# A feed-forward block's input on Trainium2: shift of odd tiles and one weight remainder on GpSimd, later statistics for the second half, another order within each product

## The chip, the core and the metric

The kernel runs on one core of a Trainium2 chip. A core has TensorE (matrix products), VectorE and ScalarE (elementwise work), GpSimd (elementwise work too) and SyncE, which issues most DMA transfers. The metric is the time of one execution on the device in microseconds (us); the lower the better.

## The reference, cut to what matters

The model has two layers on 256 latent tokens `x` and 256 context tokens `z`, with 1024 features. Each layer is a half-step feed-forward block, a token mixing, and a second half-step feed-forward block.

```python
def rms_norm(x): return x * lax.rsqrt(mean(x * x, axis=-1) + EPS)
def modulate(h, shift, scale): return h * (1.0 + scale) + shift
def swiglu(h, w1, w3, w2): return (silu(h @ w1) * (h @ w3)) @ w2      # D_FF = 2816

for l in range(2):
    last = l == 1
    x = x + 0.5 * mx[2] * swiglu(modulate(rms_norm(x), mx[0], mx[1]), ffn1_w1[l], ffn1_w3[l], ffn1_w2[l])
    z = z + 0.5 * mz[2] * swiglu(modulate(rms_norm(z), mz[0], mz[1]), ffn1_w1[l], ffn1_w3[l], ffn1_w2[l])
    hx, hz = (modulate(rms_norm(x), mx[3], mx[4]) @ w_in[l], modulate(rms_norm(z), mz[3], mz[4]) @ w_in[l])
    mix_x, mix_z = token_mixing(hx, hz, ...)      # Fourier, neighbourhood attention, GLA, grouped attention
    x = x + mx[5] * (mix_x @ w_out[l])
    x = x + 0.5 * mx[8] * swiglu(modulate(rms_norm(x), mx[6], mx[7]), ffn2_w1[l], ffn2_w3[l], ffn2_w2[l])
    if not last: ...                              # the same two steps for z
return x
```

`mx` and `mz` are nine vectors of 1024 (shift, scale and gate of each block), computed from `c` and `c_ctx` by a matrix product. The token mixing is not touched by the change other than where it calls the common product.

## The kernel before

**Layout.** The state stands transposed in SBUF: eight tiles `X[d]` of 128 features by 512 columns. Columns 0 to 255 are the latents (first half, `s = 0`), 256 to 511 the context (second half, `s = 1`). The second feed-forward block of layer 1 works on the latents alone.

**Products in three parts.** All large products are made at near-f32 precision out of rounded operands (`fp32r`). Of a weight tile `raw` (128 x 1024, streamed in by SyncE's DMA queue in the order of `wlist`, three buffers), ScalarE casts the rounded high part `whi` (line 234) and VectorE subtracts for the remainder `wlo` (line 237). The activations stand as `hh` and `hl` in the same way. `mm3` (lines 278 to 280) then gives `product` (line 266; the matmul is line 271) three matmuls for each product: `whi` by `hh`, `whi` by `hl`, `wlo` by `hh`. Weights are prepared up to `LEAD = 2` ahead of use.

**The feed-forward block.** `ffn` (line 386) handles 22 tiles of 128 hidden features in two groups of 12 and 10. The first two tiles of a block, each with a `w1` and a `w3` product, so four weights, are interleaved: first all products of both tiles for the latents, and then all for the context. So the first products need the latents' tiles `hh0`, `hl0`, `hh1`, ... one after the other, and the context's only later. After that each product is 512 columns wide. The block's last two output tiles are done half by half (`SPLIT = 2`), so that the latents' state is complete earlier; `out_proj` of the mixing (line 1052) does the same (`SPLITO = 2`).

**From one block into the next.** After each output tile `norm_square` (line 283) squares it on ScalarE (`sq`) and adds it to the running sum `ss`, on GpSimd (line 298), for the last tile on VectorE. When a half's last tile is done, `norm_stat` (line 303) is called after a number of further products: a matmul with ones sums over the features (line 310), VectorE scales it to `ms` (line 318), GpSimd raises it to the power -0.5, `rs` (line 320). Some products later `norm_bcast` (line 324) spreads `rs` over the partitions with two transposes into the PSUM tile `pb` (line 327). The table `LAGS` holds both numbers for the two halves: `((6, 6), (4, 4))` means statistics 6 products after a half's last square, broadcast 4 products after that, for either half; its keys 3, 6 and 0 are the block that is entered (mixing, second and first feed-forward block). Where only the latents are computed, there are no lags.

Then `norm_apply_` (line 339) makes the activation tiles of the half, d = 0 to 7, through four buffers `htmp`: VectorE forms `htmp` = X times scale times `pb` (line 347), and ScalarE adds the shift and rounds for `hh` (line 349). For an even tile VectorE makes `hl` from `htmp`, shift and `hh` in one instruction (line 354). For an odd tile (`POOLD`) ScalarE adds the shift to `htmp` in place (line 351), and GpSimd subtracts `hh` (line 352).

**What sets the order.** The program is written unit by unit. A scheduler, which holds its own simulated timeline, puts the instructions of each engine in order, by priority (`tc.high_priority`), and the products are kept behind statistics and broadcasts by `issue_after` and `keep_in_program_order`. Each engine then executes its list strictly in that order. Beside all this VectorE works through `mod_module` (line 159), the vectors of the later blocks, as background work pinned behind the `wlo` instruction recorded last.

## Time and profile before

| | before |
|---|---|
| device time, three runs | 1767.90, 1768.75, 1769.67 us |
| their median | 1768.75 us |
| the profiled execution | 1767.38 us |
| its span in the profile | 1765.6 us |
| granted TensorE clock, mean over the span | 0.989 of full |
| share of the span busy: TensorE, VectorE, ScalarE, GpSimd | 97%, 62%, 38%, 12% |

The profile is of one execution. The span runs from its first to its last recorded instruction; the device time of the same execution is 1.8 us longer. An engine's busy share is a mean over the whole program, in which the feed-forward blocks and the mixing alternate. The granted clock tells at which share of its full speed TensorE was allowed to run.

### The profile page before, as it was taken

Reading aid. Unit: us, or ns where it says so; the run is one execution under the profiler, and the core shown is the slowest. Engines: PE = TensorE matmul, PEld = TensorE weight load, DVE = VectorE, ACT = ScalarE, POOL = GpSimd, SP = SyncE. Lnnn points to the kernel's source line nnn. Section 1 sums busy time; section 2 is a strip of 40 time slices with the busy share of each in tenths; the row PEclk is TensorE's granted clock in tenths of the full one; section 3 lists DMA queues with packets and bytes.
Section 4 is the critical chain, followed back from the end, with each engine's and each line's share of the span. In section 5 each row is a group of like instructions: output and inputs, shape, how many; then the busy total and the mean of one; then the engine's idle time right before and its main releaser. Section 6 shows DMA issues by size and latency. Waiting matters only on the chain.

```text
span 1765.6 us, 27971 instructions
## 1 busy us (share of the span) xinstructions
PE 1708.3 (97%) x11142; PEld 1477.1 (84%) x11142; DVE 1100.2 (62%) x1832; ACT 667.3 (38%) x1122; POOL 216.5 (12%) x259
## 2 busy tenths in 40 slices
PE   7999999999989999999999999999999897999999
PEld 5888888887978788888888888888888796889999
DVE  4577877645876668777333478778733576655554
ACT  4422222235645453222222352222223464554443
POOL 1000000022553230000000110000001344120000
PEclk9999999999999999999999999999999998999999
DMA  9555765333221046655332366567523333136664
GB/s 337 185 186 156 225 203 179 122 94 106 75 62 34 30 150 187 197 166 175 108 98 68 100 212 213 168 198 222 167 81 99 91 103 82 49 124 193 182 190 136
DMA packets 92275, 254.03 MB, mean 144 GB/s; under 512 B 17649, under 2 KB 28145, under 8 KB 91761
## 3 DMA queue, kind: packets, MB, share of 16 engines
q1 hardware_dynamic: 90560, 250.93, 46.0%
q8 instruction: 87, 1.43, 0.3%
q10 hardware_dynamic: 1584, 1.32, 0.2%
q14 instruction: 44, 0.35, 0.1%
HBM read 251.16 MB, written 1.05 MB: 143 GB/s over the span
## 4 chain that ended last, share of the span: by engine, by line
PE 89%; DMA 4%; DVE 3%; ACT 1%; issue 1%; POOL 1%; SPq 0%; POOLq 0%; DVEq 0%; ACTq 0%
PE p L271 48%; PE py L271 23%; PE pt L271 8%; PE pyo L271 3%; DMA bias<-in_na_rpb_dram 2%; PE pf L271 1%; PE po L776 1%; PE prT L767 1%; DVE wlo L237 1%; PE sc L744 1%; DMA wfirst<-in_wmodf_dram 1%; PE pa L660 1%; PE pg L540 0%; ACT whi L234 0%; DMA raw<-in_f1w_dram 0%
## 5 line engine op out<-in xcount | busy, mean ns | idle before, releaser
L234 ACT CAST whi<-raw 128x1024 fp32r<-128x1024 f32 (+3 forms) x358 | 340.0, 951 | 893.5 <-PE p L271 289.2
L237 DVE TENSOR_TENSOR wlo<-raw,whi 128x1024 fp32r<-128x1024 f32 (+3 forms) x358 | 396.6, 1110 | 226.6 <-ACT whi L234 219.0
L271 PE MATMUL p<-hl,whi 128*128 128x512 f32 (+1 forms) x1504 | 527.5, 352 | 2.1 <-DVE hl L354 1.4
L271 PE MATMUL p<-hh,wlo 128*128 128x512 f32 (+1 forms) x1504 | 526.7, 351 | 0.3 <-DVE wlo L237 0.3
L271 PE MATMUL p<-hh,whi 128*128 128x512 f32 (+1 forms) x1504 | 524.9, 352 | 1.9 <-ACT hh L349 1.1
L271 PEld LDWEIGHTS p<-hl,whi 128*128 128x128 f32 x1504 | 285.2, 190 | 40.5 <-DVE hl L354 1.8
L271 PEld LDWEIGHTS p<-hh,whi 128*128 128x128 f32 x1504 | 283.6, 190 | 40.9 <-ACT hh L349 1.9
L271 PEld LDWEIGHTS p<-hh,wlo 128*128 128x128 f32 x1504 | 285.2, 190 | 38.4 <-DVE wlo L237 0.6
L167 DVE CUSTOM_DVE_ANT_0 mprod<-wmod,crow 128x1024 f32<-128x1024 f32 x256 | 301.9, 1218 | 0.0
L271 PE MATMUL py<-gh,whi 128*128 128x512 f32 (+1 forms) x764 | 266.3, 350 | 0.0
L271 PE MATMUL py<-gh,wlo 128*128 128x512 f32 (+1 forms) x764 | 265.7, 348 | 0.0
L271 PE MATMUL py<-gl,whi 128*128 128x512 f32 (+1 forms) x764 | 264.0, 346 | 0.0
L298 POOL TENSOR_TENSOR ss<-ss,sq 128x512 f32<-128x512 f32 (+1 forms) x34 | 40.9, 1202 | 1064.6 <-ACT sq L295 1063.1
L396 DVE TENSOR_TENSOR g<-p,sl 128x512 f32<-128x512 f32 (+1 forms) x88 | 54.9, 624 | 180.6 <-PE p L271 180.1
L271 PEld LDWEIGHTS py<-gh,wlo 128*128 128x128 f32 x764 | 143.4, 188 | 20.5
L271 PEld LDWEIGHTS py<-gl,whi 128*128 128x128 f32 x764 | 143.3, 188 | 19.8
L271 PEld LDWEIGHTS py<-gh,whi 128*128 128x128 f32 x764 | 143.5, 188 | 17.7
L271 PE MATMUL pt<-whi,hl 128*128 128x256 f32 x448 | 132.7, 296 | 9.7 <-POOL hl L352 9.7
L271 PE MATMUL pt<-whi,hh 128*128 128x256 f32 x448 | 132.6, 296 | 1.2 <-ACT nt L518 0.7
L271 PE MATMUL pt<-wlo,hh 128*128 128x256 f32 x448 | 132.3, 295 | 0.0
L466 DVE SCALAR_TENSOR_TENSOR X<-py,mod,X 128x256 f32<-128x256 f32 x112 | 50.3, 480 | 98.6 <-PE py L271 98.5
L271 PEld LDWEIGHTS pt<-whi,hl 128*128 128x128 f32 x448 | 88.7, 198 | 18.5 <-POOL hl L352 12.5
(218 smaller groups left out, 1706.9 us busy)
## 6 DMA issues: line engine op xcount, KB each, us to landing
wmod<-in_wmodt_dram SPq DMA_DIRECT2D x128, 512.0 KB, 3.7
raw<-in_f1w_dram SPq DMA_DIRECT2D x88, 512.0 KB, 4.1
raw<-in_f2w_dram SPq DMA_DIRECT2D x88, 512.0 KB, 4.1
raw<-in_f1w_dram SPq DMA_DIRECT2D x32, 384.0 KB, 3.7
raw<-in_f2w_dram SPq DMA_DIRECT2D x32, 384.0 KB, 3.4
raw<-in_f1w_dram SPq DMA_DIRECT2D x32, 320.0 KB, 2.8
raw<-in_f2w_dram SPq DMA_DIRECT2D x32, 320.0 KB, 2.9
wfirst<-in_wmodf_dram SPq DMA_DIRECT2D x32, 256.0 KB, 5.9
```

Of the source, the lines that this page charges most:

```text
L167: nc.vector.tensor_tensor_reduce(out=prod, in0=raw, in1=crow[:, s], scale=1.0, scalar=0.0, op0=ALU.mult, op1=ALU.add, accum_out=acc[:, s, ...
L234: nc.scalar.copy(hi[:, :k * n], raw[:, :k * n])
L237: wlo[0] = nc.vector.tensor_tensor(out=lo[:, :k * n], in0=raw[:, :k * n], in1=hi[:, :k * n].bitcast(F32), op=ALU.subtract).ins
L271: nc.tensor.matmul(ps, w, x, start=first and i == 0, stop=last and i == len(parts) - 1)
L298: (nc.vector if d == KD - 1 else eng).tensor_tensor(out=st["ss"][:, c], in0=st["ss"][:, c], in1=sq[:, c], op=ALU.add)
L396: nc.vector.tensor_tensor(out=g[:, :n], in0=p3[:, :n], in1=sl[:, :n], op=ALU.mult)
L466: nc.vector.scalar_tensor_tensor(out=X[mt][:, c], in0=py[:, c], scalar=mcol(l, m, mt, s), in1=X[mt][:, c], op0=ALU.mult, op1=ALU.add)
L660: nc.tensor.matmul(pa[w * b:w * b + w, c * w:c * w + w], ke[hs, k0:k0 + w], qe[hs, q0:q0 + w], start=True, stop=True)
L744: nc.tensor.matmul(ps[:, :n], q[:, e, (t % 2) * P:(t % 2 + 1) * P], ks[e][:, T - n:T], start=i == 0, stop=i == 1)
L767: nc.tensor.transpose(pt[:, c * P:(c + 1) * P], pr[e][:, (2 * half + i) * P:(2 * half + i + 1) * P], ident)
L776: last_mm = nc.tensor.matmul(po[64 * e:64 * e + 64, c0:c0 + P], vs[e][4 - nkt + kt], prT[:, (2 * e + i) * P:(2 * e + i + 1) * P], start=kt ...
```

## The change

The diff makes four edits.

1. In `norm_apply_`, the shift of odd tiles goes from ScalarE to GpSimd (`tensor_scalar` with the shift as a column), except on entry to the mixing (`m == 3`) and to the very first block (`l + m == 0`). These are the entries to the second feed-forward block of layer 0 and to the first of layer 1, with two halves, and to the second of layer 1, with the latents alone: 8 + 8 + 4 instructions.
2. In the same three blocks the fourth weight (`w3` of the second tile, noted in `plow`) gets its remainder `wlo` on GpSimd instead of VectorE. That instruction is not recorded in `wlo[0]`.
3. `LAGS` for the entries 6 and 0: the second half's statistics come 14 products after its last square instead of 6.
4. `mm3` takes `wlo` by `hh` second and `whi` by `hl` last. This holds for every product that goes through `mm3`.

```diff
--- before.py
+++ after.py
@@ -23,7 +23,7 @@
 EPS = 1e-6
 LEVELS = (64, 32, 16, 8, 4, 2, 1)
 LEAD = 2
-LAGS = {3: ((6, 6), (4, 4)), 6: ((6, 6), (4, 4)), 0: ((6, 6), (4, 4))}
+LAGS = {3: ((6, 6), (4, 4)), 6: ((6, 14), (4, 4)), 0: ((6, 14), (4, 4))}
 SPLIT = 2
 SPLITO = 2
 SKIP = 4
@@ -178,9 +178,12 @@
 
 
     wlist = []
+    plow = []
 
     def ffn_units(l, f):
         w1, w3, w2 = a[f"f{f}w1"], a[f"f{f}w3"], a[f"f{f}w2"]
+        if l or f == 2:
+            plow.append(len(wlist) + 3)
         for f0, f1 in ((0, FA), (FA, NF)):
             for t in range(f0, f1):
                 wlist.append((w1[l, t], KD, 128))
@@ -218,23 +221,26 @@
     def w_load():
         if pos[0] < len(wlist):
             src, k, n = wlist[pos[0]]
+            low = nc.gpsimd if pos[0] in plow else nc.vector
             pos[0] += 1
             raw = wp.tile([P, 1024], F32, tag="raw", name="raw", bufs=3)
             nc.sync.dma_start(out=raw[:, :k * n], in_=src)
-            loaded.append((raw, k, n))
+            loaded.append((raw, k, n, low))
 
     def w_conv(pool=None, after=None):
         if not loaded:
             w_load()
         if not loaded:
             return
-        raw, k, n = loaded.pop(0)
+        raw, k, n, low = loaded.pop(0)
         tp, nb = (wp, 4) if pool is None else (pool, 1)
         hi = tp.tile([P, 1024], F32R, tag="whi", name="whi", bufs=nb)
         nc.scalar.copy(hi[:, :k * n], raw[:, :k * n])
         lo = tp.tile([P, 1024], F32R, tag="wlo", name="wlo", bufs=nb)
         with tc.issue_after(after) if after is not None else nullcontext():
-            wlo[0] = nc.vector.tensor_tensor(out=lo[:, :k * n], in0=raw[:, :k * n], in1=hi[:, :k * n].bitcast(F32), op=ALU.subtract).ins
+            i = low.tensor_tensor(out=lo[:, :k * n], in0=raw[:, :k * n], in1=hi[:, :k * n].bitcast(F32), op=ALU.subtract).ins
+        if low is nc.vector:
+            wlo[0] = i
         ready.append((hi[:, :k * n].rearrange("p (k n) -> p k n", k=k),
                       lo[:, :k * n].rearrange("p (k n) -> p k n", k=k),
                       raw[:, :k * n].rearrange("p (k n) -> p k n", k=k)))
@@ -277,7 +283,7 @@
 
     def mm3(ps, w, k, xh, xl, first, last):
         wh, wl = w[:2]
-        product(((wh[:, k, :], xh), (wh[:, k, :], xl), (wl[:, k, :], xh)), ps, first, last)
+        product(((wh[:, k, :], xh), (wl[:, k, :], xh), (wh[:, k, :], xl)), ps, first, last)
 
 
     def norm_square(st, pool, d, s0, s1, eng=nc.gpsimd):
@@ -348,7 +354,10 @@
                                            in1=st["pb", s][:, :S], op0=ALU.mult, op1=ALU.mult)
             nc.scalar.activation(hh[:, c], tmp, AF.Identity, bias=mcol(l, m, d, s))
             if d in POOLD[s]:
-                nc.scalar.activation(tmp, tmp, AF.Identity, bias=mcol(l, m, d, s))
+                if m == 3 or l + m == 0:
+                    nc.scalar.activation(tmp, tmp, AF.Identity, bias=mcol(l, m, d, s))
+                else:
+                    nc.gpsimd.tensor_scalar(out=tmp, in0=tmp, scalar1=mcol(l, m, d, s), scalar2=None, op0=ALU.add)
                 nc.gpsimd.tensor_tensor(out=hl[:, c], in0=tmp, in1=hh[:, c].bitcast(F32), op=ALU.subtract)
             else:
                 st["hl", s, d] = nc.vector.scalar_tensor_tensor(out=hl[:, c], in0=tmp, scalar=mcol(l, m, d, s),
```

The scheduler turns this into the following orders. A row is the line of the code, the operation and its tiles (result <- operands, with running numbers) and its size. `ss` is the running sum of squares, `rs` the power, `hl1` to `hl7` the low activations of the odd tiles, `p13` the result of an interleaved product, `pb` the PSUM tile of the statistics. The diff moves line numbers by 4 to 9.

GpSimd on entry to the second feed-forward block of layer 0, before:

```order
L298 TENSOR_TENSOR ss_6152<-ss_6152,sq_6366 128x256
L320 TENSOR_TENSOR rs_6428<-ms_6426,mhalf_94 128x2
L298 TENSOR_TENSOR ss_6152<-ss_6152,sq_6437 128x256
L352 TENSOR_TENSOR hl1_6456<-htmp_6457,hh1_6455 128x256
L352 TENSOR_TENSOR hl3_6469<-htmp_6470,hh3_6468 128x256
L352 TENSOR_TENSOR hl5_6482<-htmp_6483,hh5_6481 128x256
L320 TENSOR_TENSOR rs_6565<-ms_6563,mhalf_94 128x2
L352 TENSOR_TENSOR hl7_6495<-htmp_6496,hh7_6494 128x256
```

GpSimd at the same place, after:

```order
L326 TENSOR_TENSOR rs_6428<-ms_6426,mhalf_94 128x2
L304 TENSOR_TENSOR ss_6152<-ss_6152,sq_6437 128x256
L360 TENSOR_SCALAR htmp_6457<-htmp_6457,mod0_97 128x256
L360 TENSOR_SCALAR htmp_6470<-htmp_6470,mod0_97 128x256
L361 TENSOR_TENSOR hl1_6456<-htmp_6457,hh1_6455 128x256
L241 TENSOR_TENSOR wlo_6540<-raw_6536,whi_6538 128x1024
L361 TENSOR_TENSOR hl3_6469<-htmp_6470,hh3_6468 128x256
L360 TENSOR_SCALAR htmp_6483<-htmp_6483,mod0_97 128x256
L360 TENSOR_SCALAR htmp_6496<-htmp_6496,mod0_97 128x256
L361 TENSOR_TENSOR hl5_6482<-htmp_6483,hh5_6481 128x256
L361 TENSOR_TENSOR hl7_6495<-htmp_6496,hh7_6494 128x256
L326 TENSOR_TENSOR rs_6589<-ms_6587,mhalf_94 128x2
```

Four shifts (line 360) and the fourth weight's remainder `wlo_6540` have come into the row. The remainder stands between `hl1` and `hl3`, two shifts now stand ahead of `hl1`, and the second power `rs_6589`, which stood ahead of `hl7`, now stands behind it.

TensorE at the same entry, around the second half's statistics (the matmul with ones), before:

```order
L271 MATMUL p13_6527<-hh3_6468,whi_6371 128x256
L271 MATMUL p13_6527<-hl3_6469,whi_6371 128x256
L271 MATMUL p13_6527<-hh3_6468,wlo_6373 128x256
L271 MATMUL p13_6527<-hh4_6475,whi_6371 128x256
L310 MATMUL pb_6560<-ones_92,ss_6152 128x1 x2
L271 MATMUL p13_6526<-hh3_6468,whi_6336 128x256
L271 MATMUL p13_6526<-hl3_6469,whi_6336 128x256
L271 MATMUL p13_6526<-hh3_6468,wlo_6338 128x256
```

TensorE around the same statistics, after:

```order
L277 MATMUL p13_6527<-hl6_6489,whi_6371 128x256
L316 MATMUL pb_6584<-ones_92,ss_6152 128x1 x2
L277 MATMUL p13_6526<-hh7_6494,whi_6336 128x256
L277 MATMUL p13_6526<-hh7_6494,wlo_6338 128x256
L277 MATMUL p13_6527<-hh7_6494,whi_6371 128x256
L277 MATMUL p13_6527<-hh7_6494,wlo_6373 128x256
L277 MATMUL p13_6528<-hh0_6449,whi_6532 128x256
L277 MATMUL p13_6528<-hh0_6449,wlo_6534 128x256
L277 MATMUL p13_6528<-hl0_6450,whi_6532 128x256
L277 MATMUL p13_6529<-hh0_6449,whi_6538 128x256
L277 MATMUL p13_6529<-hh0_6449,wlo_6540 128x256
```

The statistics stood between the products of tiles 3 and 4 and now stand between those of tiles 6 and 7. Within each product `wlo` now comes ahead of `hl`. The remainder made on GpSimd, `wlo_6540`, is first used in the last row here, by the fourth product (`p13_6529`). The entry to the first feed-forward block of layer 1 is ordered alike.

GpSimd on entry to the second feed-forward block of layer 1 (latents alone), before:

```order
L298 TENSOR_TENSOR ss_14238<-ss_14238,sq_14412 128x256
L298 TENSOR_TENSOR ss_14238<-ss_14238,sq_14447 128x256
L320 TENSOR_TENSOR rs_14491<-ms_14489,mhalf_94 128x2
L352 TENSOR_TENSOR hl1_14502<-htmp_14503,hh1_14501 128x256
L352 TENSOR_TENSOR hl3_14515<-htmp_14516,hh3_14514 128x256
L352 TENSOR_TENSOR hl5_14528<-htmp_14529,hh5_14527 128x256
L352 TENSOR_TENSOR hl7_14541<-htmp_14542,hh7_14540 128x256
```

GpSimd at the same place, after:

```order
L304 TENSOR_TENSOR ss_14238<-ss_14238,sq_14412 128x256
L304 TENSOR_TENSOR ss_14238<-ss_14238,sq_14447 128x256
L241 TENSOR_TENSOR wlo_14565<-raw_14561,whi_14563 128x1024
L326 TENSOR_TENSOR rs_14491<-ms_14489,mhalf_94 128x2
L360 TENSOR_SCALAR htmp_14503<-htmp_14503,mod1_98 128x256
L360 TENSOR_SCALAR htmp_14516<-htmp_14516,mod1_98 128x256
L361 TENSOR_TENSOR hl1_14502<-htmp_14503,hh1_14501 128x256
L361 TENSOR_TENSOR hl3_14515<-htmp_14516,hh3_14514 128x256
L360 TENSOR_SCALAR htmp_14529<-htmp_14529,mod1_98 128x256
```

Here the remainder `wlo_14565` stands between the last sum of squares and the power, and the shifts stand in pairs ahead of the `hl` that need them.

## Rows read from the trace of the kernel before

**Rows 1.** Page part 1: busy us (share) and instructions of each engine.

```profile
PE 1708.3 (97%) x11142; PEld 1477.1 (84%) x11142; DVE 1100.2 (62%) x1832; ACT 667.3 (38%) x1122; POOL 216.5 (12%) x259
```

**Rows 2.** Windows: stretch, length, busy us per engine, granted clock, DMA share, GB/s.

```profile
644.00:656.00 12.00, 9.51 (x79) 9.10 (x78) 9.70 (x20) 8.09 (x16) 4.09 (x6) 1.00 0.26 79
1009.00:1021.00 12.00, 9.53 (x80) 9.11 (x78) 10.95 (x19) 9.03 (x16) 4.34 (x5) 1.00 0.55 191
1567.00:1574.00 7.00, 4.75 (x23) 4.32 (x24) 5.69 (x13) 4.07 (x11) 2.20 (x3) 0.66 0.44 141
```

**Rows 3.** TensorE's timeline, gap 1: start, us, instruction, [idle us ahead, releaser].

```profile
649.04 0.40 PE L271 MATMUL p<-hh,whi 128*128 128x256 f32 x2
...
650.82 0.38 PE L271 MATMUL p<-hl,whi 128*128 128x256 f32 x1 [1.38 <-DVE hl L354]
...
654.58 0.61 PE L310 MATMUL pb<-ones,ss 128*128 128x1 f32 x4 [1.11 <-DVE ss L298]
```

**Rows 4.** TensorE's timeline, gap 2.

```profile
1015.22 0.40 PE L271 MATMUL p<-hh,whi 128*128 128x256 f32 x2
1015.46 0.36 PE L271 MATMUL p<-hl,whi 128*128 128x256 f32 x1
...
1017.16 0.38 PE L271 MATMUL p<-hl,whi 128*128 128x256 f32 x1 [0.75 <-POOL hl L352]
...
1020.86 0.60 PE L310 MATMUL pb<-ones,ss 128*128 128x1 f32 x4 [1.71 <-DVE ss L298]
```

**Rows 5.** TensorE's timeline, gap 3.

```profile
1568.97 0.43 PE L327 MATMUL pb<-cst,rs 128*128 128x128 f32 x2 [1.04 <-POOL rs L320]
```

**Rows 6.** VectorE's timeline, ahead of and in gap 1, ahead of gap 2.

```profile
628.67 1.60 DVE L237 TENSOR_TENSOR wlo<-raw,whi 128x1024 fp32r<-128x1024 f32 x1 [1.57 <-ACT whi L234]
...
647.10 1.66 DVE L347 SCALAR_TENSOR_TENSOR htmp<-X,mod,pb 128x256 f32<-128x256 f32 x4 [0.45 <-PE pb L327]
...
648.67 1.22 DVE L237 TENSOR_TENSOR wlo<-raw,whi 128x1024 fp32r<-128x1024 f32 x1
649.80 1.35 DVE L354 SCALAR_TENSOR_TENSOR hl<-htmp,mod,hh 128x256 fp32r<-128x256 f32 x2
...
1013.76 1.22 DVE L237 TENSOR_TENSOR wlo<-raw,whi 128x1024 fp32r<-128x1024 f32 x1
```

**Rows 7.** ScalarE's timeline, gap 1 and ahead of gap 3.

```profile
647.61 1.36 ACT L349 ACTIVATE hh<-htmp,mod 128x256 fp32r<-128x256 f32 x3 [0.20 <-DVE htmp L347]
...
648.88 0.49 ACT L351 ACTIVATE htmp<-htmp,mod 128x256 f32<-128x256 f32 x1
...
1565.69 1.04 ACT L234 CAST whi<-raw 128x1024 fp32r<-128x1024 f32 x1 [1.06 <-PE pyo L271]
```

**Rows 8.** GpSimd's timeline, ahead of and in gap 1, in gap 3.

```profile
627.89 1.30 POOL L298 TENSOR_TENSOR ss<-ss,sq 128x512 f32<-128x512 f32 x1
629.30 2.12 POOL L298 TENSOR_TENSOR ss<-ss,sq 128x512 f32<-128x512 f32 x1
...
649.45 1.03 POOL L352 TENSOR_TENSOR hl<-htmp,hh 128x256 fp32r<-128x256 f32 x1 [1.23 <-ACT htmp L351]
...
1568.21 0.71 POOL L320 TENSOR_TENSOR rs<-ms,mhalf 128x2 f32<-128x2 f32 x1 [2.05 <-DVE ms L318]
```

**Rows 9.** Page part 5, groups: instruction, count | busy, mean ns | idle ahead.

```profile
L271 PE MATMUL p<-hl,whi 128*128 128x512 f32 (+1 forms) x1504 | 527.5, 352 | 2.1 <-DVE hl L354 1.4
L271 PE MATMUL p<-hh,wlo 128*128 128x512 f32 (+1 forms) x1504 | 526.7, 351 | 0.3 <-DVE wlo L237 0.3
```

**Rows 10.** Single lines: count, ns (least/median/longest), first and last start.

```profile
L352 POOL TENSOR_TENSOR hl<-htmp,hh x44: 717/745/1888, 23.8 to 1575.4; 128x256 fp32r<-128x256 f32 x44
L796 POOL CAST qhi<-qhi x24: 391/474/1274, 449.6 to 1501.5; 64x256 fp32r<-64x256 f32 x24
L842 POOL MEMSET bias<- x4: 312/314/316, 395.1 to 1382.2; 128x256 f32 x4
L354 DVE SCALAR_TENSOR_TENSOR hl<-htmp,mod,hh x44: 468/479/968, 23.0 to 1574.0; 128x256 fp32r<-128x256 f32 x44
```

## The prediction

> **What bounds the kernel now.** I read the page's busy shares first: TensorE is busy for 1708.3 of the 1765.6 us [rows 1], so a change that leaves its work alone can win only its waits. The windows show where the three handovers into FFN halves lie: in 644 to 656 us it is busy for 9.51 of 12.00 us, in 1009 to 1021 for 9.53 [rows 2]. I call these gap 1 (FFN 2 of layer 0) and gap 2 (FFN 1 of layer 1); gap 3 (FFN 2 of layer 1, latents alone) is near 1567. The TensorE timeline splits the idle time. Gap 1: 1.38 us for VectorE's `hl` of tile 0, 1.11 us for the sum of squares of the second half [rows 3]. Gap 2: 0.75 for GpSimd's `hl` and 1.71 for the sum of squares [rows 4]. Gap 3: a serial chain, with 1.04 us for GpSimd's power among it [rows 5]. So all that the change can remove is 2.49 + 2.46 us and part of gap 3, 0.3% of the time. What the reader should look at next is who makes tiles while TensorE waits: VectorE, ScalarE and GpSimd share one chain there [rows 6 to 8], and VectorE and GpSimd don't run freely beside each other.
>
> **They block each other.** A GpSimd sum of squares (128x512) ran from 627.89 for 1.30 us. A VectorE `wlo` that began at 628.67 took 1.60 us, where one that nothing holds takes 1.22; the next GpSimd sum began at 629.30 and took 2.12 [rows 6, 8]. Each stretched by about what was left of the other: 628.67 + 1.60 is 629.19 + 1.1, and 629.30 + 2.12 is 630.2 + 1.2. In gap 1 GpSimd's `hl` asked at 649.45, while `wlo` held VectorE to about 649.8, and went first; VectorE's two `hl` then took 1.35 us [rows 6, 8] instead of some 0.9. I therefore let two operations that both read SBUF tensors twice (VectorE) or at all (GpSimd) run one after the other, in the order in which they ask. Reads from PSUM (`htmp`, the evictions) run beside GpSimd.
>
> **The change, part by part.**
>
> The order of the three products costs nothing in itself: `hl,whi` takes 352 ns and `hh,wlo` 351 [rows 9], and their number stays. It takes the wait for `hl` behind `hh,wlo`, which in the interleaved first pair buys two matmuls, 2 x 0.12 us (two of them lie between 1015.22 and 1015.46 [rows 4]).
>
> The statistics 8 products later take away the waits for `ss`, 1.11 and 1.71 us. Behind the second broadcast the program keeps 26 matmuls of the first half, 3.1 us, while in gap 1 the first `hh` began 0.5 us after the first `htmp`, and `hl` 0 ended within 3.7 us of it (647.10, 647.61, 649.80 [rows 6, 7]) with a `wlo` between that is absent in the second half. The second half is covered; no cost.
>
> The shift goes from ScalarE (0.49 us each [rows 7]) to GpSimd: 8 + 8 + 4 instructions. No one-input operation of 128x256 with a column operand is in the trace. Bounds: a MEMSET of that size, 314 ns, and the two-input `hl`, 745 [rows 10]. A one-input CAST of 64x256, median 474, is nearest; I take 0.47. The Trainium skill (GPSIMD Engine Reference, section 4.1, Engine selection) says that GpSimd is about twice as slow as VectorE with two inputs but roughly at line rate with one. By that an add would cost near the MEMSET's 0.31, and the sum below would be 1.3 us lower; the CAST row speaks for the larger price.
>
> The low half on GpSimd: 128x256 takes 0.745 and 128x512 1.30 [rows 8, 10], so 0.555 for each 256 columns and, as an estimate, 1.30 + 2 x 0.555 = 2.4 us for 128x1024, where VectorE needed 1.22 [rows 6]. What decides is its place: in gaps 1 and 2 it stands on GpSimd's queue ahead of the `hl` of tiles 3, 5 and 7, which TensorE needs sooner than this weight, whose first product stands after all the first pair's; in gap 3 it stands ahead of the power.
>
> **Gap 1, step by step**, with the starts of rows 6 to 8 as they are up to the fourth `htmp`. GpSimd's first add runs 648.6 to 649.05; VectorE's `wlo` waits for it and ends at 650.2; the second add asked at 649.45 and runs to 650.6; `hl` of tile 0 follows, to 651.05. TensorE has done four products by 649.7 (649.04 + 3 x 0.12 + 0.28): 1.4 us idle, as much as before. GpSimd's `hl` 1 ends at 651.8, in time. VectorE's `hl` 2 asked before GpSimd's `wlo`, and ends at 652.2; `wlo` runs 652.2 to 654.55. VectorE's sum of squares has asked by then and goes first, to 655.0; `hl` 3 ends at 655.7. TensorE, 14 products of 0.12 on from 651.1 with the last ending at 653.4, waits 2.3 us. Then `hl` 4 (VectorE) to 656.15, the add for tile 5 to 656.6, `hl` 6 to 657.0, and only now VectorE's `htmp` 7, since it stands behind `hl` 6: 657.4; `hh` 7 to 657.95; its add, which stands ahead of `hl` 5, to 658.5; `hl` 5 to 659.2. TensorE ran out at 657.35: 1.9 us. Together 1.4 + 2.3 + 1.9 = 5.6 against 2.49: **+3.1 us**.
>
> **Gap 2**, the same way from the `wlo` at 1013.76 [rows 6] and TensorE's first product at 1015.22 [rows 4]: add to 1015.4, `hl` 0 to 1015.9 (no wait), `hl` 1 to 1016.55, a VectorE `wlo` to 1017.7, the second add to 1018.1, `hl` 2 to 1018.55 against TensorE ready at 1017.55 (1.0 us), GpSimd's `wlo` to 1020.9, the sum of squares, `hl` 3 to 1022.0 against 1019.5 (2.5), `hl` 5 to 1025.45 against 1023.65 (1.9). 5.4 against 2.46: **+2.9 us**.
>
> **Gap 3**: the fourth weight's `whi` is cast from 1565.69 for 1.04 us, so GpSimd's `wlo` runs 1566.8 to 1569.15, and the power, which began at 1568.21 [rows 7, 8], begins at 1569.15: **+0.95 us**. VectorE's saved `wlo` ended at the time `ms` was ready anyway.
>
> **Sum**: +3.1 + 2.9 + 0.95 = +6.95 us, on the profiled execution's 1767.38 (span 1765.6) 1774.3. The median of the runs shown is 1768.75, 1.4 above it, so 1775.7.
>
> **Rivals.**
> - *The waits go, as the edits say.* If GpSimd's `wlo` were out of the way of `hl` 3, the gaps would keep the 1.38 and 0.75 us at most, less 2 x 0.12 each, and the 1.11 and 1.71 for `ss` would be gone: 2.8 + 0.5 = 3.3 us off, and 4.95 with the `hl` waits gone too. In the middle, 4.2 off, 1764.5. It decides at one point: `hl` 3 must be there when TensorE has done tile 2, at 652.8 to 653.4 in gap 1. With `hl` 1 ending at 651.8, that leaves GpSimd 0.9 us beside `hl` 3's own 0.74. Only a `wlo` of under 0.2 us, or one that runs before `hl` 1, fits. Chance 0.08.
> - *The engines don't block each other here.* Then `hl` 0 comes at 650.3, GpSimd does its adds, `hl` 1, `wlo` and `hl` 3 back to back from 649.45 and ends at about 653.8, and waits of 0.6 + 1.1 replace 2.49 in gap 1: -0.8 there, as much in gap 2, +0.95 in gap 3: 1768. Rows 8 speak against it. Halfway cases (a cheaper add, `hl` 3 ahead of the sum of squares) fall between this and the sum. Chance of ending within 0.2%, 0.17.
> - *The clock falls as well.* In 1567 to 1574, after the waits of gap 3, the granted clock is 0.66, a mix of its two levels, 2.4 and 1.2 GHz, while in gaps 1 and 2, idle for 2.5 of 12 us, it stays at 1.00 [rows 2]. With 5.5 us idle there a fall is possible: 4.75 us busy of 7 at 0.66 cost some 2 us more than at full clock, so 1778 to 1780 for one or two of them. The Trainium skill (TensorE: Matmul & The Clock Gate, Part 1) ties the gate to how busy the engine has been of late; the three windows agree. Chance 0.15.
> - *GpSimd is dearer than taken*: an add at 0.74 us, as for two inputs, adds 0.27 to each of about six serial adds, 1.6 us and as much by what queues behind: 1778 to 1779. Chance 0.10.
>
> **How the numbers follow.** The sum itself, 1771 to 1778, has 0.50. About 0.2%, 3.5 us, is what a measurement of this kernel can tell from no change. Faster 0.08 is the first rival; within 0.2% 0.17 is the second; the rest, 0.75, is slower. The range leaves out most of the faster case below and two clock falls together with a dear add above: 1768 to 1781.
>
> **What would show it.** In the profile after: no TensorE wait for `ss` in gaps 1 and 2 (the statistics were right); a GpSimd `wlo` of 2.2 to 2.8 us in each gap, and TensorE's longest wait there named after GpSimd's `hl` 3 or 5, or VectorE's `hl` 2 or 4 behind it; TensorE busy for some 3 us less than before in windows from the first norm product to 16 us on; the power of gap 3 behind `wlo`. Wrong, if `hl` 3 is there before TensorE, if `wlo` on GpSimd takes under 1.5 us, or if VectorE's subtractions show their 0.48 us [rows 10] beside GpSimd's.

## The result, and the profile after

The changed kernel takes 1780.89 us in the median (1777.82 to 1783.35, 4 runs), against 1768.33 for the kernel before (4 runs): 1.0070 of it, with an interval of 1.0051 to 1.0089. It is slower by 12.6 us. The forecast was 1775.7, in a range of 1768.0 to 1781.0: the direction was right, and the time lies at the very upper end of the range; two of the four executions lie above it.

The profiled execution took 1783.35 us (span 1781.5, 15.9 more than before). The page's first part, with the columns of [rows 1]:

```profile
PE 1716.2 (96%) x11142; PEld 1482.4 (83%) x11142; DVE 1104.4 (62%) x1829; ACT 656.0 (37%) x1102; POOL 247.9 (14%) x282
```

GpSimd got 23 instructions and 31.4 us more: 20 shifts and 3 low halves. ScalarE and VectorE lost those. TensorE is *busy* for 8 us more with the same 11142 matmuls, which already says that they took longer somewhere. TensorE's timeline, the rows on which it waits, in gap 1, gap 2 and gap 3:

```profile
653.52 0.50 PE L277 MATMUL p<-hl,whi 128*128 128x256 f32 x2 [0.66 <-DVE hl L363]
655.84 0.62 PE L277 MATMUL p<-hl,whi 128*128 128x256 f32 x2 [1.35 <-POOL hl L361]
659.04 0.69 PE L277 MATMUL p<-hl,whi 128*128 128x256 f32 x2 [0.44 <-POOL hl L361]
662.58 0.50 PE L277 MATMUL p<-hl,whi 128*128 128x256 f32 x2 [1.66 <-POOL hl L361]
...
1024.44 0.51 PE L277 MATMUL p<-hl,whi 128*128 128x256 f32 x2 [0.75 <-POOL hl L361]
1028.71 0.80 PE L277 MATMUL p<-hl,whi 128*128 128x256 f32 x2 [2.58 <-POOL hl L361]
1032.26 0.79 PE L277 MATMUL p<-hl,whi 128*128 128x256 f32 x2 [0.61 <-POOL hl L361]
...
1585.41 0.69 PE L333 MATMUL pb<-cst,rs 128*128 128x128 f32 x2 [1.94 <-POOL rs L326]
```

The number in brackets is the wait, and behind it stands what ended it. No row waits for a sum of squares any more. What was 1.38 + 1.11 us in gap 1 [rows 3] is 4.11, what was 0.75 + 1.71 in gap 2 [rows 4] is 3.94, and nearly all of it is for GpSimd's `hl` (of tiles 1, 3 and 5 in both gaps, by their place in TensorE's order). GpSimd's timeline, gap 1 and gap 3:

```profile
651.85 3.24 POOL L360 TENSOR_SCALAR htmp<-htmp,mod 128x256 f32<-128x256 f32 x2 [0.33 <-ACT hh L355]
655.06 0.73 POOL L361 TENSOR_TENSOR hl<-htmp,hh 128x256 fp32r<-128x256 f32 x1
655.74 2.37 POOL L241 TENSOR_TENSOR wlo<-raw,whi 128x1024 fp32r<-128x1024 f32 x1
658.07 0.91 POOL L361 TENSOR_TENSOR hl<-htmp,hh 128x256 fp32r<-128x256 f32 x1
658.96 1.10 POOL L360 TENSOR_SCALAR htmp<-htmp,mod 128x256 f32<-128x256 f32 x1
...
1582.35 2.34 POOL L241 TENSOR_TENSOR wlo<-raw,whi 128x1024 fp32r<-128x1024 f32 x1 [1.10 <-ACT whi L238]
1584.65 0.71 POOL L326 TENSOR_TENSOR rs<-ms,mhalf 128x2 f32<-128x2 f32 x1
1587.66 2.15 POOL L360 TENSOR_SCALAR htmp<-htmp,mod 128x256 f32<-128x256 f32 x2 [2.31 <-ACT hh L355]
```

From 651.85 on GpSimd has no pause until 660: two shifts, `hl` 1, the low half, `hl` 3, a shift. When nothing holds it, one shift takes 1.0 to 1.1 us behind another instruction of GpSimd's, and 0.92 after a pause. In gap 3 the power follows directly on the low half. VectorE's timeline at the same places:

```profile
651.85 1.22 DVE L241 TENSOR_TENSOR wlo<-raw,whi 128x1024 fp32r<-128x1024 f32 x1
652.99 1.01 DVE L363 SCALAR_TENSOR_TENSOR hl<-htmp,mod,hh 128x256 fp32r<-128x256 f32 x2
...
656.22 2.17 DVE L304 TENSOR_TENSOR ss<-ss,sq 128x256 f32<-128x256 f32 x1
658.32 1.57 DVE L363 SCALAR_TENSOR_TENSOR hl<-htmp,mod,hh 128x256 fp32r<-128x256 f32 x2
...
1587.71 1.02 DVE L363 SCALAR_TENSOR_TENSOR hl<-htmp,mod,hh 128x256 fp32r<-128x256 f32 x2
```

The sum of squares, 0.41 us alone, took 2.17: it ended 0.3 us behind GpSimd's low half (655.74 + 2.37). `hl` 4 and 6 behind it took 1.57 instead of 0.9, beside GpSimd's `hl` 3.

A second part of the loss is the clock. Windows of the kernel after, with the columns of [rows 2]:

```profile
655.00:660.00 5.00, 3.72 (x18) 3.43 (x19) 4.35 (x6) 1.23 (x3) 5.00 (x5) 0.66 0.34 102
...
1027.00:1032.00 5.00, 2.93 (x12) 2.64 (x12) 2.95 (x4) 2.02 (x2) 4.15 (x5) 0.61 1.01 412
1032.00:1037.00 5.00, 4.74 (x22) 4.75 (x23) 0.16 (x1) 0.29 (x1) 1.62 (x3) 0.50 0.34 138
1037.00:1042.00 5.00, 5.00 (x39) 5.00 (x39) 1.78 (x5) 1.26 (x4) 0.25 (x1) 0.86 0.00 0
```

and of the kernel before, as far behind the first product of gap 2 (1015.22 there, 1022.19 here) as the window from 1032:

```profile
1025.00:1030.00 5.00, 5.00 (x44) 5.00 (x43) 4.03 (x9) 4.59 (x12) 2.24 (x3) 1.00 0.41 166
```

After the waits the granted clock stands at 0.50, the lower of its two levels (1.2 of 2.4 GHz), and 22 matmuls fill the time of 44. Busy time times what is missing of the clock gives an estimate of the loss: 3.72 x 0.34 = 1.3 us in gap 1, and 2.93 x 0.39 + 4.74 x 0.50 + 5.00 x 0.14 = 4.2 us in gap 2, together 5.5.

### The profile page after: what moved, and what is told of

The parts are those of the page before. It is cut to its first block, busy times and chain, and to the rows that moved or that the text cites. A ratio compares the mean times of both kernels' runs of the same rounds, so it can differ in the third digit from the quotient of the medians.

```text
span 1781.5 us, 27930 instructions
## 1 busy us (share of the span) xinstructions
PE 1716.2 (96%) x11142; PEld 1482.4 (83%) x11142; DVE 1104.4 (62%) x1829; ACT 656.0 (37%) x1102; POOL 247.9 (14%) x282
## 4 chain that ended last, share of the span: by engine, by line
PE 89%; DMA 3%; DVE 3%; ACT 1%; POOL 1%; issue 1%; SPq 0%; POOLq 0%; DVEq 0%; ACTq 0%
PE p L277 47%; PE py L277 23%; PE pt L277 8%; PE pyo L277 4%; DMA bias<-in_na_rpb_dram 2%; PE pf L277 1%; PE po L785 1%; PE prT L776 1%; DVE wlo L241 1%; PE sc L753 1%; ACT whi L238 1%; PE pg L549 1%; PE pa L669 1%; DMA raw<-in_f1w_dram 0%; DMA wfirst<-in_wmodf_dram 0%
## 5 line engine op out<-in xcount | busy, mean ns | idle before, releaser
L277 PEld LDWEIGHTS p<-hh,whi 128*128 128x128 f32 x1504 | 287.7, 191 | 40.8 <-ACT hh L355 2.0
L403 ACT ACTIVATE sl<-p 128x512 f32<-128x512 f32 (+1 forms) x88 | 47.9, 545 | 252.0 <-PE p L277 251.9
```

Of the source, the lines that this page charges most:

```text
L277: nc.tensor.matmul(ps, w, x, start=first and i == 0, stop=last and i == len(parts) - 1)
L403: nc.scalar.activation(sl[:, :n], p1[:, :n], AF.Silu)
```

## The experiments

For each kernel the table has the median, its ratio to the runs of the kernel before on the same chip, TensorE's waits in gaps 1 and 2 (the sum of the bracketed times, as above), and the stretch: from the end of the first half's power on GpSimd to the end of the block's tenth gate product on VectorE, summed over both gaps, less the same of before (117.45 + 118.81 us). The stretch is free of what happens elsewhere in the program, and it includes the clock. Waits and stretch are of one profiled execution for each kernel. The ratio is taken over all runs, so it can differ a little from that of the medians.

| kernel | median, us | ratio (95%) | waits, gaps 1 / 2 | stretch |
|---|---|---|---|---|
| before, in the four comparisons | 1768.3 to 1769.4 | 1 | 2.49 / 2.46 | 0 |
| after, first comparison | 1780.89 | 1.0070 (1.0051 to 1.0089) | 4.11 / 3.94 | +9.8 |
| after, repeated (e0) | 1779.11 | 1.0060 (1.0048 to 1.0072) | 5.36 / 5.15 | +10.0 |
| low half back on VectorE (e1) | 1772.98 | 1.0018 (1.0009 to 1.0027) | 2.52 / 2.10 | +2.0 |
| shift back on ScalarE (e2) | 1771.02 | 1.0010 (1.0000 to 1.0019) | 2.26 / 2.38 | -0.6 |
| both back (e3) | 1771.31 | 1.0010 (1.0001 to 1.0019) | 2.56 / 2.35 | -0.4 |
| late statistics alone (e4) | 1770.18 | 0.9999 (0.9988 to 1.0010) | 2.81 / 2.83 | +2.1 |
| product order alone (e5) | 1770.29 | 1.0006 (0.9996 to 1.0016) | 2.35 / 2.16 | -0.7 |
| e4, two instructions pinned (e8) | 1769.93 | 1.0007 (0.9997 to 1.0017) | 2.72 / 2.46 | +0.4 |
| after, waits filled (e9) | 1778.70 | 1.0053 (1.0039 to 1.0068) | 2.07 / 1.13 | +7.2 |
| after, low half last (e10) | 1772.82 | 1.0018 (1.0009 to 1.0027) | 2.00 / 2.04 | +2.0 |
| after, shift with two inputs (e11) | 1775.14 | 1.0038 (1.0025 to 1.0050) | 3.05 / 3.18 | +2.1 |
| after, old lags (e13) | 1776.33 | 1.0040 (1.0025 to 1.0056) | 3.79 / 2.98 | +5.0 |
| late statistics, low half last on GpSimd (e12) | 1765.39 | 0.9982 (0.9971 to 0.9992) | 1.38 / 1.31 | -1.6 |

**Repeated.** No edit.

> The changed kernel unaltered, beside the other runs of this set, so that they can be compared on one chip. Waits of 5 to 6 us in gaps 1 and 2 each, and TensorE's matmuls 0.21 us apart instead of 0.12 for some microseconds behind the longest wait. 1778 to 1783 if the result of the first comparison holds. If the granted clock falls in only some executions, its times spread over 4 us or more.

1779.11 us. The loss is as before, divided otherwise: longer waits, and less time at the low clock. The windows in which the clock stood lowest:

```profile
660.00:665.00 5.00, 4.21 (x23) 4.21 (x24) 0.16 (x1) 0.00 (x0) 2.17 (x4) 0.68 0.00 0
...
1032.00:1037.00 5.00, 5.00 (x31) 5.00 (x32) 0.16 (x1) 0.00 (x1) 1.33 (x2) 0.69 0.47 193
```

By the same estimate that is 2.9 us. So the waits grew by 3.1 us and the clock took 5.5 in the first profiled execution, 5.6 and 2.9 in this one, and the stretch is nearly the same (9.8 and 10.0). One can stand for the other: the wait for `hl` 3 in gap 1 is 0.44 us where TensorE came to it at the low clock, and 1.51 here, where the clock was still at 1.00.

**Low half back on VectorE**, from the changed kernel:

```diff
-            plow.append(len(wlist) + 3)
+            pass
```

> The changed kernel with the fourth weight's low half back on VectorE; shift on GpSimd, late statistics and product order stay. Theory A (the prediction's: the 2.36 us low half in front of hl 3 on GpSimd's queue carries the loss): the waits of gaps 1 and 2 fall from 5.1 and 4.8 us to about the 2.5 of before, the clock stays at 1.00 there, time 1768 to 1771. Theory B (GpSimd's adds carry it: 1.07 us each where 0.47 was taken): waits stay at 4 us or more in each gap, 1774 to 1779. Theory C (neither alone: GpSimd is simply given more than the first pair's 6 to 12 us hold, each piece costs about 2 us alone): 1770 to 1772. In all of them the power of gap 3 comes 0.9 us earlier again.

1772.98 us, between the ranges of theories C and B: 6 to 9 us of the loss go. The waits are together as long as before, but in gap 1 they are 0.66 us for `hl` 0 and 1.86 for `hl` 1, which stands behind both shifts on GpSimd; those for `hl` 3 and 5 are gone. What is left in the gaps, 2.0 us, is mostly the clock, which still fell behind that wait (4.00 x 0.33 = 1.3 us). Its window:

```profile
655.00:660.00 5.00, 4.00 (x21) 4.00 (x22) 3.11 (x8) 1.82 (x4) 4.61 (x6) 0.67 0.50 166
```

**Shift back on ScalarE**, from the changed kernel:

```diff
-                if m == 3 or l + m == 0:
+                if True:
                     nc.scalar.activation(tmp, tmp, AF.Identity, bias=mcol(l, m, d, s))
```

> The changed kernel with the odd tiles' shift back on ScalarE; low half on GpSimd, late statistics and product order stay. Theory A: the low half still stands in front of hl 3, so nearly all of the loss stays, 1776 to 1781. Theory B: the loss goes, 1768 to 1770, with GpSimd's power in gap 3 still 0.9 us late. Theory C: 1769.5 to 1772, with one wait of 1 to 2.5 us behind the low half in each gap and a granted clock of 1.00.

1771.02 us. Theory A fails here: the low half still stands ahead of `hl` 3, and the stretch is not longer than before. TensorE waits for `hl` 3 behind the low half, but for no more than it waited anyway:

```profile
654.81 0.50 PE L277 MATMUL p<-hl,whi 128*128 128x256 f32 x2 [1.11 <-POOL hl L361]
...
1020.86 0.50 PE L277 MATMUL p<-hl,whi 128*128 128x256 f32 x2 [1.72 <-POOL hl L361]
```

So each of the two moves costs 2 us of the stretch or nothing by itself, and both together cost 10: nearest to theory C.

**Both back** (the two diffs above together):

> Shift and low half both back where they were; only the later statistics of the second half and the product order stay. Rival 1 of the prediction's gain, without GpSimd's new work: the waits for the sum of squares (1.11 and 1.71 us) go and nothing takes their place, 1764 to 1766. Theory C with the waits moved: TensorE reaches hl 4 by as much earlier as it no longer waits for the statistics, VectorE's sum of squares stands ahead of hl 4 all the same, and the wait comes back there under another name: 1767.5 to 1769.

1771.31 us, above both ranges, and a stretch as before. The prediction's gain isn't there even without new work for GpSimd.

**Late statistics alone** (the same, with the old order in `mm3`):

> The kernel before with the later statistics of the second half alone, in the old product order. If the waits for the sum of squares simply go: 1765 to 1766.5. If they come back at hl 4, behind VectorE's sum of squares: 1768 to 1769.5, no more than 0.05% from before. Product order is the difference to the run with both: 0 to 0.6 us.

1770.18 us: no gain, and no difference to before (0.9999). Most of the longer stretch is clock, which fell to 0.66 behind a wait of 2.07 us in gap 2 (4.38 us busy in that window of 5, so 1.5 us). The wait for the sum of squares is gone and stands at `hl` 4 under another name. TensorE, VectorE and GpSimd in gap 1:

```profile
655.04 0.39 PE L277 MATMUL p<-hl,whi 128*128 128x256 f32 x1 [1.43 <-DVE hl L363]
```

```profile
651.93 1.21 DVE L241 TENSOR_TENSOR wlo<-raw,whi 128x1024 fp32r<-128x1024 f32 x1
...
653.45 0.75 DVE L304 TENSOR_TENSOR ss<-ss,sq 128x256 f32<-128x256 f32 x1
654.12 0.47 DVE L353 SCALAR_TENSOR_TENSOR htmp<-X,mod,pb 128x256 f32<-128x256 f32 x1
654.52 0.87 DVE L363 SCALAR_TENSOR_TENSOR hl<-htmp,mod,hh 128x256 fp32r<-128x256 f32 x2
```

```profile
649.12 1.04 POOL L361 TENSOR_TENSOR hl<-htmp,hh 128x256 fp32r<-128x256 f32 x1 [1.23 <-ACT htmp L358]
650.86 0.75 POOL L361 TENSOR_TENSOR hl<-htmp,hh 128x256 fp32r<-128x256 f32 x1 [0.71 <-ACT htmp L358]
653.18 0.74 POOL L361 TENSOR_TENSOR hl<-htmp,hh 128x256 fp32r<-128x256 f32 x1 [1.57 <-ACT htmp L358]
655.88 0.74 POOL L361 TENSOR_TENSOR hl<-htmp,hh 128x256 fp32r<-128x256 f32 x1 [1.96 <-ACT htmp L358]
```

The last fence also suggests why the two moves don't add up simply. GpSimd has 1.23 + 0.71 + 1.57 + 1.96 = 5.5 us of pauses here. Four shifts of 1.09 are 4.4 us, the low half is 2.4: by this rough count either fits, and both (6.8) don't.

**Product order alone** (the kernel before with the new order in `mm3`). Expected were 1768.5 to 1769 us if the order costs nothing, and 1770 to 1771.5 if it costs what some traces had suggested. It took 1770.29, by 1.0006 (0.9996 to 1.0016) not to be told from before; in the gaps the stretch is 0.7 us shorter.

**Two instructions pinned.** From the kernel with late statistics alone, VectorE's sum of squares and the fourth weight's low half (on VectorE) behind `hl` 6 of the first half (the lines that note `hl` 6 and the weight are left out):

```diff
...
+            late = st.get(("hl", 0, 6)) if d == KD - 1 and s0 and st.get("lag") and st["lag"][1] > 6 else None
+            with tc.issue_after(late) if late is not None else nullcontext():
                 (nc.vector if d == KD - 1 else eng).tensor_tensor(out=st["ss"][:, c], ...)
...
+        if low and lateh[0] is not None:
+            after, lateh[0] = lateh[0], None
...
```

> The kernel with the late statistics alone (old product order, nothing on GpSimd), and VectorE's sum of squares and low half of the fourth weight pinned behind hl 6 of the first half in gaps 1 and 2. Theory: with late statistics alone the wait came back at hl 4 (1.65 and 2.29 us) because these two instructions stand ahead of it on VectorE's queue; behind hl 6 they are still in time. Then only the wait for hl 0 (gap 1, 1.6) and hl 1 (gap 2, 1.0) stays: 1765 to 1767 against 1769.4 for the kernel before. Rival: the wait at hl 4 is due to its hh, late by a whi cast on ScalarE, and the pins only shift it: 1768.5 to 1770.5.

1769.93 us, no gain. The wait moved once more, to GpSimd's `hl` 5. TensorE, GpSimd and VectorE:

```profile
655.77 0.39 PE L279 MATMUL p<-hl,whi 128*128 128x256 f32 x1 [1.35 <-POOL hl L365]
```

```profile
653.52 2.89 POOL L365 TENSOR_TENSOR hl<-htmp,hh 128x256 fp32r<-128x256 f32 x2 [1.82 <-ACT htmp L362]
```

```profile
653.59 0.41 DVE L308 TENSOR_TENSOR ss<-ss,sq 128x256 f32<-128x256 f32 x1
653.92 1.22 DVE L244 TENSOR_TENSOR wlo<-raw,whi 128x1024 fp32r<-128x1024 f32 x1
```

GpSimd's two `hl` are 1.48 us of work and took 2.89. They were asked while VectorE's `hl` 6 still ran (to 653.66), and VectorE's two instructions behind that were not held at all. The expectation had both reasons wrong: neither the pinned instructions nor `hh` decides alone; what fits is the time that VectorE and GpSimd need one after the other.

**Waits filled.** From the changed kernel, matmuls whose result is overwritten later, ahead of the products of the tiles for which TensorE waited (`lastm` is the matmul before):

```diff
+FILL = {6: {1: 9, 3: 7, 5: 12}, 0: {1: 6, 2: 16, 5: 12}}
...
+                            if l + m and n > S and i == 0 and f == 0:
+                                for _ in range(FILL[m].get(k, 0)):
+                                    with tc.issue_after(lastm[0]):
+                                        nc.tensor.matmul(ps[1, 0][:, c], ws[0, 0][0][:, k, :], h[k - 1][0][:, c], start=True, stop=True)
```

> The changed kernel with 62 more matmuls (28 in gap 1, 34 in gap 2; 0.12 us each, 7.4 us of added work) whose result is overwritten: 9, 7 and 12 right ahead of the products of tiles 1, 3 and 5 in gap 1, and 6, 16 and 12 ahead of those of tiles 1, 2 and 5 in gap 2, where TensorE waited for hl 1.0 to 2.8 us. Theory: the waits stay as long but TensorE spends them working; the granted clock no longer falls behind them (0.50 to 0.71 for some 5 to 8 us), matmuls stay 0.12 us apart, and the time falls by 3 to 6 us although work was added: 1773 to 1776 against 1779.1. Rival (the halved rate behind the waits has another cause, such as the operands' arrival): the added work costs what doesn't fit into the waits, 1779 to 1783.

The added work cost nothing, but the expected 3 to 6 us didn't come either: 1778.70 us against 1779.11. In the profiled execution the clock held, as the theory has it. Windows of that run:

```profile
655.00:660.00 5.00, 4.31 (x37) 4.11 (x36) 3.48 (x4) 0.54 (x2) 4.15 (x4) 1.00 0.38 105
...
1027.00:1032.00 5.00, 4.56 (x37) 4.36 (x37) 1.24 (x3) 2.32 (x2) 3.36 (x4) 1.00 1.03 421
1032.00:1037.00 5.00, 5.00 (x44) 5.00 (x44) 1.33 (x4) 0.66 (x2) 0.73 (x1) 1.00 0.04 17
```

Its span is 3.8 us below that of the repeated run, 2.8 of them in the gaps. The medians are 0.4 us apart, with intervals of 2 us and more on each. So in these two executions the clock stayed up when TensorE's idle time was filled, and the fall's price in the gaps is some 3 us; that the time as a whole gains by filling is not shown.

**Low half last.** From the changed kernel, GpSimd's low half pinned behind `hl` 7 in gaps 1 and 2:

```diff
...
+        if low is not nc.vector and lateh[0] is not None:
+            after, lateh[0] = lateh[0], None
...
-                nc.gpsimd.tensor_tensor(out=hl[:, c], in0=tmp, in1=hh[:, c].bitcast(F32), op=ALU.subtract)
+                i = nc.gpsimd.tensor_tensor(out=hl[:, c], in0=tmp, in1=hh[:, c].bitcast(F32), op=ALU.subtract).ins
+                if d == 7 and s == 0 and st.get("lag") and st["lag"][1] > 6:
+                    lateh[0] = i
```

> The changed kernel with GpSimd's low half pinned behind hl 7 of the first half in gaps 1 and 2 (gap 3 as it is): the same work for GpSimd, in another place. Theory A (place): the wait for hl 3 goes and the low half is at most 1 to 2 us late for the fourth product, waits of 3.4 and 4.0 instead of 5.3 and 5.5 us, and without the fall of the clock 1771 to 1775. Theory C (amount): the same work has to be done before the fourth product anyway, and what is won at hl 3 is lost there, 1777 to 1782.

1772.82 us: the same work in another place takes 6 us less. TensorE's longest wait in gap 1, for `hl` 1, and the one for the low half in gap 2:

```profile
655.36 0.63 PE L280 MATMUL p<-hl,whi 128*128 128x256 f32 x2 [1.34 <-POOL hl L364]
...
1029.57 0.39 PE L280 MATMUL p<-hh,wlo 128*128 128x256 f32 x1 [0.19 <-POOL wlo L244]
```

So place decides after all, once the shift is on GpSimd: TensorE asks for the low half last. The 2.0 us of the stretch that are left are as many as with the low half on VectorE, and the wait for `hl` 1 behind the shifts is left in both.

**Shift with two inputs**, from the changed kernel:

```diff
-                    nc.gpsimd.tensor_scalar(out=tmp, in0=tmp, scalar1=mcol(l, m, d, s), scalar2=None, op0=ALU.add)
+                    nc.gpsimd.tensor_tensor(out=tmp, in0=tmp, in1=bc(mcol(l, m, d, s), S), op=ALU.add)
```

> The changed kernel with GpSimd's shift written as a two-input add of htmp and the shift column spread over 256 columns, in place of the add with a column operand (1.07 us each when nothing holds it). If the column form is what is dear: 0.72 to 0.75 us each, as the subtraction of hl, and 20 x 0.33 us less for GpSimd; 1774 to 1778 if that counts. If the two-input form holds VectorE as GpSimd's other two-input operations do (VectorE's sum of squares took 2.17 us beside the low half), what is won on GpSimd is lost on VectorE, 1778 to 1783. If a spread column costs the same as a column operand, 1.07 us, no change.

1775.14 us, 4 us less. The form with a column operand is the dear one. Single lines, after and here (count, ns least/median/longest, first and last start):

```profile
L360 POOL TENSOR_SCALAR htmp<-htmp,mod x20: 917/1087/2330, 651.9 to 1592.5; 128x256 f32<-128x256 f32 x20
```

```profile
L360 POOL TENSOR_TENSOR htmp<-htmp,mod x20: 607/716/1706, 651.5 to 1582.9; 128x256 f32<-128x256 f32 x20
```

The scheduler also put the second shift behind `hl` 1 here; how much of the 4 us that is was not tried apart.

**Old lags**, from the changed kernel:

```diff
-LAGS = {3: ((6, 6), (4, 4)), 6: ((6, 14), (4, 4)), 0: ((6, 14), (4, 4))}
+LAGS = {3: ((6, 6), (4, 4)), 6: ((6, 6), (4, 4)), 0: ((6, 6), (4, 4))}
```

> The changed kernel with the statistics of the second half back at 6 products. If the later statistics gained what the prediction gave them (2.8 us), the time rises by 2 to 3 us, 1781 to 1783. If the first half's hl are what TensorE waits for either way, the waits for the sum of squares run inside that time, and it stays within 1 us of 1779.1, or falls, since VectorE is asked for the second half's tiles sooner and the longest wait is cut in two: 1776 to 1779.

1776.33 us. In the gaps' stretch the late statistics cost 5 us where they were to gain 2.8; the whole times are 2.8 us apart, with intervals that overlap (1.0025 to 1.0056, 1.0048 to 1.0072). TensorE's waits with the old lags:

```profile
658.08 0.61 PE L316 MATMUL pb<-ones,ss 128*128 128x1 f32 x4 [1.17 <-DVE ss L304]
660.84 0.43 PE L333 MATMUL pb<-cst,rs 128*128 128x128 f32 x2 [0.62 <-POOL rs L326]
...
1025.73 1.01 PE L316 MATMUL pb<-ones,ss 128*128 128x1 f32 x4 [2.23 <-DVE ss L304]
```

There is none for `hl` 5. The order of TensorE's products says why. Here, behind the second broadcast (gap 1):

```
L333 MATMUL pb_6560<-cst_72,rs_6565 128x128 x2
L277 MATMUL p13_6526<-hh5_6481,whi_6336 128x256
L277 MATMUL p13_6526<-hh5_6481,wlo_6338 128x256
L277 MATMUL p13_6528<-hh0_6449,whi_6532 128x256
L277 MATMUL p13_6528<-hh0_6449,wlo_6534 128x256
L277 MATMUL p13_6528<-hl0_6450,whi_6532 128x256
```

It goes on like this: 31 matmuls of the second pair of weights, 3.7 us, stand in the first pair's products between the last of `hh` 5 and the first of `hl` 5. In the changed kernel `hl` 5 comes directly behind the four matmuls of `hh` 5, all products of tiles 5 and 6 stand ahead of the statistics, and those of the second pair of weights come later.

**Late statistics, low half last on GpSimd.** What the runs point to: shift on ScalarE, old product order, late statistics, and the low half on GpSimd behind `hl` 7, in gaps 1 and 2 alone. From the kernel of "low half last":

```diff
-        if l or f == 2:
+        if l + f == 2:
             plow.append(len(wlist) + 3)
...
-                if m == 3 or l + m == 0:
+                if True:
...
-        product(((wh[:, k, :], xh), (wl[:, k, :], xh), (wh[:, k, :], xl)), ps, first, last)
+        product(((wh[:, k, :], xh), (wh[:, k, :], xl), (wl[:, k, :], xh)), ps, first, last)
```

> Late statistics in the old product order, shift on ScalarE, and in gaps 1 and 2 alone the fourth weight's low half on GpSimd, pinned behind hl 7 of the first half (gap 3 keeps it on VectorE). If place is what decides, VectorE is free of that low half ahead of hl 4 and GpSimd does it when TensorE no longer asks for hl: the wait of 1.65 and 2.29 us at hl 4 shrinks to some 0.5 to 1 each, with up to 0.5 for the low half itself: 1766.5 to 1768.5. If the two engines' shared time before hl 7 is the bound, as the run with both pins on VectorE suggests, a wait of about 1.5 us stays under another name: 1769 to 1770.5.

1765.39 us, 0.9982 of before (0.9971 to 0.9992): it beats both kernels, if by little, and lies 1.1 us below the better of the two ranges. Whether the late statistics are needed for it was not tried. Gap 1 has one wait left, gap 2 two (the second is shown), and GpSimd does the low half when nothing else is asked of it:

```profile
650.12 0.39 PE L280 MATMUL p<-hl,whi 128*128 128x256 f32 x1 [1.38 <-DVE hl L368]
...
1018.64 0.39 PE L280 MATMUL p<-hl,whi 128*128 128x256 f32 x1 [0.56 <-DVE hl L368]
```

```profile
654.81 2.38 POOL L244 TENSOR_TENSOR wlo<-raw,whi 128x1024 fp32r<-128x1024 f32 x1
```

## Why the prediction came out as it did

**Direction and mechanism: right.** GpSimd's new work makes its `hl` late, TensorE waits there, and no wait for the sum of squares is left. The waits forecast as 5.6 and 5.4 us came out as 4.11 and 3.94, and as 5.36 and 5.15 in the repeated run. Not all of them are where they were forecast. In gap 1 they were to be 1.4 us for `hl` 0, 2.3 for `hl` 3 and 1.9 for `hl` 5, with `hl` 1 "in time"; they were 0.66, 0.44 and 1.66, and 1.35 for `hl` 1, which stood behind both shifts. (The 14 products counted there up to 653.4 are 18: 14 bring TensorE to 652.8, where it starts on `hh` 3. The 2.3 us stand.) The low half took 2.35 us where 2.4 was worked out. In gap 3 the power waited 1.94 us against 1.04 [rows 5]: +0.90, forecast +0.95.

**The size: in the range, in part by luck.** +7.0 us was forecast, and +12.6 came. Between the two profiled executions the waits of gaps 1 and 2 grew by 3.1 us where 6.0 were in the sum. The clock, about 5.5 us, was not in it, nor were the 5 us outside of the three gaps.

**The shift's price: wrong.** 0.47 us was taken, between bounds of 0.31 and 0.745 [rows 10]; it is 0.92 after a pause and 1.09 in the median. The bounds were taken from rows without a column operand, and the price lies outside them. The two-input form, which the prediction held for the dearer one, takes 0.61 at the least and 0.72 in the median. The rule of the Trainium skill that was weighed there (GPSIMD Engine Reference, section 4.1, Engine selection: roughly line rate with one input) would have been further off, and the trace speaks against it for this form.

**The blocking: right for two inputs, too wide for one.** VectorE's sum of squares (2.17 us) shows it. But two shifts took 2.15 us, 1.07 each, beside two `hl` of VectorE that took 1.02 (0.87 alone, in the run with late statistics): neither held the other by more than 0.15 us, though the prediction let every GpSimd read of SBUF hold them. Behind VectorE's `wlo` the shifts did wait (3.24 for two). The dearer shift and the milder blocking worked against each other, which helped the sum of the waits to come out near. The Trainium skill (SBUF — State Buffer, Who interferes with whom) says that a VectorE instruction with two SBUF inputs contends with a GpSimd instruction that reads SBUF; for this pair, by 1.02 us against 0.87, that is hardly so.

**The later statistics: wrong.** "The second half is covered; no cost" looked at the second half. The cost was in the first: when the late statistics alone take the waits for `ss` away (e4), they come back at `hl` 4, and beside GpSimd's new work the later statistics leave TensorE nothing to do ahead of `hl` 5, where with the old lags (e13) 31 matmuls stand.

**"What decides is its place": half right.** The low half ahead of `hl` 3 costs nothing while GpSimd has pauses to take it (e2), and 6 to 9 us when the shifts have filled them (e1, e10).

**The clock: seen, but taken for a case beside the sum.** It was a rival with a chance of 0.15 and 2 us for each fall. In the profiled execution it fell behind the waits of gaps 1 and 2, for an estimated 1.3 and 4.2 us, part of which shorter waits gave back; filling the waits gave 2.8 us of the stretch. It goes with the waits, and is a part of the sum. How far it falls differs between executions: the four of the first comparison had mean granted clocks of 0.985, 0.985, 0.988 and 0.989 at 1783.35, 1782.24, 1779.54 and 1777.82 us. The profiled one is the longest of them, so its clock loss is not that of the median.

**What is left over.** Of the 15.9 us between the two spans, the gaps' stretch is 9.8 and the power of gap 3 0.9. Before the first power the execution lost 1.9 us, on the first weights' transfers, which the change doesn't touch. The entries of the two mixings lost about 1 us each, and the rest of the mixings up to gap 3 some 1.5 more. That is open. From the end of the second half's power at the first mixing's entry to the end of the next power, the ten traces with the new product order took 0.8 to 2.1 us longer than before, the three with the old order -0.5 to 1.1; but the time of the product order alone (1.0006, 0.9996 to 1.0016) doesn't settle it. In the gaps that order gained 0.7 us, near the 0.5 forecast.

## What to carry to other kernels

Two moves onto an idle engine can each cost little and together be dear: add up what they take of the pauses in that one stage, and put what is asked for last behind what is asked for first. A wait that is removed tells nothing until the next one is found; here it went from the sum of squares to VectorE's `hl` to GpSimd's `hl`, and only less shared work ahead of it made it smaller. Pinning statistics later also pins the products ahead of them, which may have been the cover for something else.

## What the runs showed of the hardware

An add with a column operand on GpSimd took 1.09 us for 128x256 in the median (0.92 at the least), one with two inputs, of which one is a spread column, 0.72 (0.61). GpSimd's add with a column hardly held VectorE's `hl` (two in 1.02 us beside it, 0.87 alone). And VectorE can keep GpSimd waiting over several instructions in a row: in the run with two pins GpSimd's `hl` started at 653.52, while VectorE's `hl` 6 ran, and ahead of VectorE's sum of squares (653.59) and `wlo` (653.92); yet those two ran at their own 0.41 and 1.22 us. GpSimd's two `hl`, 1.48 us of work, ended 1.3 us behind them, so hardly any of it was done before.
